# A hybrid decoder step on one core: page and score buffers shared, page numbers read ahead, and a shorter page queue

## The chip, the core and the metric

The kernel runs on one core of a Trainium2 chip. A core has TensorE for matrix products (PE in the profile, PEld where it loads weights), VectorE (DVE), ScalarE (ACT), GpSimd (POOL) and SyncE (SP). SP issues nearly all transfers between HBM and the on-chip SBUF; sixteen DMA engines carry them out. The metric is the time of one execution on the device, in microseconds, as the median of several runs.

## What is computed

One layer of a decoder for a prompt of 256 tokens and, at the same time, 8 requests of 8 new tokens each with 2048 cached positions. One input projection of the 320 rows feeds three branches, and one output projection with a layer norm closes the layer:

```python
aq, ak, av, ag, iq, ik, iw, bq, bf, bi, bg, mq, mg = _in_proj(hs, w_in[l], pos_s)
a_out = _dsa_sample(aq, ak, av, iq, iw, ik, cache_k[l], cache_v[l], cache_idx_k[l], page_table)
b_o, s_s = _hgrn2(bq, bf, bi, lb, state_hgrn[l], t_s)
m_out = _mem_attend(mq, cache_mem_k[l], cache_mem_v[l])
hs_next = _merge(hs, a_out, ag, b_o, bg, m_out, mg, hgrn_norm_g[l], w_out[l], ln_g[l], ln_b[l])
```

The first branch is sparse attention: an indexer scores all cached positions, each query keeps the best 256 and attends over them. Keys, values and indexer keys of the cache lie in pages of 128 positions; `page_table` says which physical page holds which part of a request. The second branch is a gated linear recurrence, the third an attention over 256 memory tokens. The prompt goes through the same steps without a cache.

## The kernel before, in words

**Weights.** The input projection runs as 65 blocks of output columns, each in two halves of 512 KB (`wspec`, loaded by `load_w` into three `wr` buffers). Each half is split into a high and a low part (`prep`), and TensorE makes three products for each piece, xh by high, xl by high, xh by low. Behind the 53rd block lie 16 steps for the prompt's memory keys and values (`in_wm` with `in_memT`), the memory projections of the text below. The output projection, `in_wo`, comes last.

**Pages.** The 8 requests go in 4 pairs. For each pair p there are 8 units of keys (K0 to K3 in `PAGES`), then 8 units of values (V0 to V3); a unit (`unit`) uses two tiles of 1 MB, each with two pages of 512 KB, so 32 pages for a pair's keys and 32 for its values, 256 in all, and 16 more tiles' halves for the cached memory keys and values (XK, XV). A key unit multiplies padded queries with the pages and writes scores to the PSUM bank `kv`; every second unit ScalarE copies them into the score tile S[p]. `soft` turns S[p] into probabilities and frees it; a value unit multiplies these with its pages into the bank `va`. One run of such products, one or two units, between projections is a visit. Page tiles have the tag `pg` with 6 buffers, score tiles the tag `S` with 2. Both tags hold other things at other times: the input and the first weights at the start, the indexer keys (`idx_load`, tiles `ci`) until the indexer is done, the residual and norm tables at the end.

**Page numbers.** `load_pages` asks `page(e)` for a physical number: SP reads it from the table in SBUF into a register (`value_load`, with bounds 0 to 159 that are asserted), works out the address and issues the transfer.

**What sets the order.** The program order of all engines is set when the kernel is built. The class `Plan` keeps, for each engine, the queue of SP and the DMA engines, a time up to which it is planned, and for every tile when it will be written and read. Every instruction goes through `Engine.call`, which issues it and adds its planned cost; a value load costs SP 0.65, transfers run at 380 KB per us (L134). The main loop (L1958 on) lets TensorE always take the next piece that the plan holds for ready: a pair of units whose pages have landed by the plan, or the next quarter of a weight half; one unit alone if the next projection isn't ready or after a time of patience. Background work of the other branches comes in between. `loads` decides what SP issues next: first weights, if a `wr` buffer is free by the plan, then outputs, then pages, if one of 6 buffers is free, the unit is at most 2 ahead of the one that TensorE is at, and less than 8 us of transfers are planned ahead. On the chip each instruction waits for semaphores, so an instruction that the plan put too early makes its engine wait, and SP works strictly in order.

Of the kernel before, what the change touches and what calls it, by code (L numbers as in the profile page):

```python
# [27 lines left out]
PAST = 2048  # L28
# [15 lines left out]
HASTE = 2.0  # L44
CALM = 4.0
IDLE = 3.0
TABLES = {AF.Exp: "exp_ln", AF.Ln: "exp_ln", AF.Silu: "silu", AF.Sqrt: "sqrt"}
EXP_LN = 6
PORT = ("tensor_tensor", "tensor_add", "tensor_sub", "tensor_mul", "scalar_tensor_tensor", "tensor_scalar", "tensor_copy",
# [93 lines left out]
class Engine:  # L143
# [3 lines left out]
    def __getattr__(self, op):  # L147
        f = getattr(self.raw, op)
        plan, eng = self.plan, self.name

        def call(*a, **k):
            if op == "activation":
                self.load_set(TABLES.get(a[2]))
            res = f(*a, **k)  # L154
            aps = [x for x in a if isinstance(x, bass.AP)]
            outs = [v for n, v in k.items() if n in ("out", "accum_out") and isinstance(v, bass.AP)]
            ins = [v for n, v in k.items() if n not in ("out", "accum_out") and isinstance(v, bass.AP)]
            if "out" not in k and aps:
                outs.append(aps.pop(0))
            ins = aps + ins  # L160
            if op == "value_load":
                plan.t[eng] = max(plan.t[eng], plan.now) + 0.65
            elif op == "dma_start":
                plan.dma(eng, outs[0], ins[0])
            elif op == "indirect_dma_start":
                plan.dma(eng, k["out"], k["in_"])
            elif outs:
                n = max(math.prod(x.shape[1:]) for x in outs + ins)
                plan.run(eng, self.cost(op, outs, ins, n), outs, ins,
                         op in PORT and all(x.space != bass.MemoryType.PSUM for x in outs + ins))  # L170
            return res

        return call
# [52 lines left out]
def hymba_step(ctx: ExitStack, tc: tile.TileContext, I, O):  # L226
    nc = tc.nc
    plan = Plan()
# [4 lines left out]
    ctx.enter_context(tc.manual_schedule())  # L233

    uid = [0]
    BUFS = {"t": 17, "s8": 10, "pg": 6, "bp": 2, "wr": 3, "wh": 4, "wl": 4, "S": 2, "row": 4, "mA": 2, "mB": 2, "pj": 2}

    def new(shape, tag, dt=F32, p=None):
        uid[0] += 1
        bufs = BUFS.get(tag, 1)  # L240
        t = (p or pool).tile(shape, dt, name=f"{tag}_{uid[0]}", tag=tag, bufs=bufs)
        plan.slot(tag, bufs, t.tensor.name)
        if tag in ("t", "bp"):
            live[t.tensor.name] = [tag, 1]
        return t
# [18 lines left out]
    def room(k, tag="t", spare=0):  # L264
        while not has_room(k, tag, spare() if callable(spare) else spare):
            yield
# [325 lines left out]
    def prep(i, j):  # L592
# [8 lines left out]
        raw = WR[i][:, w * j:w * j + w]  # L601
        if s.get("res") and kept.index(i) < HOMES:
            if not spare_w:
                for cols, tag in ((2880, "cat0"), (2240, "cat1"), (2320, "PT"), (2048, "pg"), (2048, "pg")):
                    t = new([128, cols], tag, F32R)
                    plan.split.add(t.tensor.name)
                    spare_w.extend(t[:, 512 * k:512 * k + 512] for k in range(4))
            hi, lo = spare_w.pop(0), spare_w.pop(0)
        elif "pair" in s:
            hi, lo = s["pair"]  # L610
        elif s.get("acc") == "rest":
            if j == 0:
                s["bp"] = [new([128, 1024], "bp", F32R) for _ in range(2)]
            hi, lo = (t[:, w * j:w * j + w] for t in s["bp"])
        else:
            hi, lo = new([128, 512], "wh", F32R), new([128, 512], "wl", F32R)
            held["w"] += 1
            s["held"] = True
# [16 lines left out]
    PG = {}  # L635

    def page(e):
        return SP.value_load(ptab[0:1, e:e + 1], min_val=0, max_val=159)

    def load_pages(n, b):  # L640
        kind, p, u = punits[n]
        t = new([128, 2, 1024], "pg")
        PG[n, b] = t
        for j in range(2):
            if kind in ("XK", "XV"):
                SP.dma_start(t[:, j, :], I["c" + kind][4 * p + 2 * b + j])
            else:
                e = (2 * p + b) * 16 + 2 * u + j
                SP.dma_start(t[:, j, :], I["c" + kind.lower()][bass.ds(page(e), 1)].rearrange("o p c -> p (o c)"))

    def pair(x, hp):

# [4 lines left out]
    def unit(n):  # L657
        kind, p, u = punits[n]
        tl = [PG.pop((n, b)) for b in range(2)]
        if kind == "K":  # L660
            if u == 0:
                S[p] = new([128, PAST + NS], "S")
            if u % 2 == 0:
                st["kv"] = PS([128, 512], "kv")
            c = 256 * (u % 2)
# [46 lines left out]
    def unit_ready(n):  # L712
# [2 lines left out]
            return False  # L715
        if kind == "K":
            return u % 2 or ("aq", 7) in done and plan.slot_free("kv", 1) <= plan.now and (
                u or plan.slot_free("S", BUFS["S"]) <= plan.now and len(S) + ci_live(1) < BUFS["S"]
                and (p < BUFS["S"] or ("soft", p - BUFS["S"]) in done))
        if kind == "V":  # L720
            return ("soft", p) in done and plan.avail(PTt[p]) <= plan.now and (u < 7 or "attn" in done) and (
# [46 lines left out]
            yield  # L768

    def ci_live(k):  # L770
        return sum([0, 1, 0, 1][p] == k and ("ci", p) in st for p in range(4))

    def idx_load():

# [1 line left out]
        t = -9.0  # L776
        for sp in range(2):
            for p in (2 * sp, 2 * sp + 1):
                st["ci", p] = x = new([128, PAST], ("pg", "S")[p % 2])
                plan.split.add(x.tensor.name)  # L780
            for c in range(2):
                for f in (1, 0):
# [65 lines left out]
    def idx_sample():  # L848
# [44 lines left out]
        def stack(k):  # L893
# [8 lines left out]
            for j in range(2):  # L902
                own, other = slice(64 * j, 64 * j + 64), slice(64 - 64 * j, 128 - 64 * j)
                ACT.copy(kk[j][own], raw[own])
                DVE.tensor_sub(kk[j][other], raw[own], kk[j][own].bitcast(F32))
            if (c, f) == (1, 0):
                del st["ci", 2 * sp + a]
            return kk

# [200 lines left out]
    def soft(p):  # L1110
# [33 lines left out]
        ps = PS([128, 128])  # L1144
        PE.transpose(ps, Sp[:, PAST - 64:], ident)
        ACT.copy(PTt[p][:, 16, :], ps)
        del S[p]
        done.add(("soft", p))

# [53 lines left out]

    def cross_prompt(h):
        yield from wait("mem", ("mq", h), "attn")
        yield from room(4)
        yield need(MQ[h], st["mkT"][h])
        ps = PS([128, 2, 256])
        for tt in range(2):
# [1 line left out]
        s8 = T8()  # L1211
        DVE.tensor_reduce(s8[:, 0:2], ps, axis=AX.X, op=OP.max)
        DVE.tensor_scalar(s8[:, 2:4], s8[:, 0:2], -QS, None, op0=OP.mult)
        P = [T(256), T(256)]
        pts = [T(256), T(256)]
        free(MQ.pop(h), st["mkT"][h])
        for tt in range(2):
            ACT.activation(P[tt], ps[:, tt, :], AF.Exp, bias=s8[:, 2 + tt:3 + tt], scale=QS,
                           accum_out=s8[:, 4 + tt:5 + tt])
# [6 lines left out]
        for nt in range(2):  # L1226
            for tt in range(2):
                PE.transpose(pt[:, nt, tt, :], P[tt][:, 128 * nt:128 * nt + 128], ident)
        free(*P)
        for nt in range(2):  # L1230
            ACT.copy(pts[nt], pt[:, nt].rearrange("p a b -> p (a b)"))
        yield need(*pts)
# [668 lines left out]
    def loads():  # L1901
        nonlocal nw, npg
        while True:
# [17 lines left out]
                SP.dma_start(dst, src)  # L1921
                continue
            n, b = divmod(npg, 2)
            if (half > 46 and n < len(punits) and len(PG) + ("q" in st) + ("more" in st) + ci_live(0) < BUFS["pg"] and n <= nunit + 2
                    and plan.slot_free("pg", BUFS["pg"]) <= plan.now + 0.2 and plan.t["DMA"] < plan.now + 8):
                load_pages(n, b)
                npg += 1
                continue
# [4 lines left out]
            if n == len(punits) and nunit == n and half > n_in - 6 and ("r", 2) not in st:  # L1933
                ln_load(2)
                continue
            return

    def prep_ready(i, j):
# [175 lines left out]
```

## Time and profile before

| what | value |
|---|---|
| median of 3 runs | 876.76 us (876.49 to 877.36) |
| profiled execution, its own time | 878.17 us |
| profiled execution, span from the first to the last instruction | 876.4 us |
| granted clock of TensorE, mean | 0.998 |
| bytes moved | 266.55 MB, mean 304 GB/s |
| page transfers of keys and of values | 128 and 128, 512 KB each |

The span of one execution in 40 equal slices of 21.9 us: the busy share of each engine in tenths, where 9 is 90% or more, the share of the 16 DMA engines, and what they moved:

```profile
PE   9999999999999999999999999999999999999996
PEld 8999898878988998879888786777888878788885
DVE  6778989748789984645745563585444333943655
ACT  6445666545463444435545364444444433744432
POOL 0543562255644461322433142334222000613424
DMA  8555544899999975999999999999998999876633
GB/s 309 182 165 160 158 144 146 300 342 405 362 410 337 372 260 161 339 411 354 398 367 399 412 377 401 405 347 383 325 408 331 350 384 384 295 269 200 192 101 120
```

TensorE is busy throughout but for the last slice. The DMA engines have three phases: half busy while the indexer runs (to about 150 us), nearly full while pages are read (to about 740 us) with one dip in the sixteenth slice, and falling while the output projection runs. Most groups in this profile carry line 154, since every instruction is issued there; they are told apart by tile names, out<-in.

### The profile page before, as it was taken

To read this page: it belongs to the slowest core of one execution; us is meant where nothing else is said; L and a number is where in the kernel's file an instruction comes from. 1 tells how busy PE (TensorE), PEld (TensorE's weight loads), DVE (VectorE), ACT (ScalarE), POOL (GpSimd) and SP (SyncE) were. 2 spreads that over 40 slices of the span, in tenths; PEclk is the share of its full clock that TensorE was granted. 3 is DMA by queue.
4 is the path that set the end of the run, shared out by engine and by line. 5 is a ranking of instruction groups with operands and counts; after the bars stand their busy time and mean duration, and the time that the engine had idled before them with its cause. 6 is when DMAs were issued, how large, how long until landed. Compare 5 with 4: busy or idle time off the path is not lost.

```text
span 876.4 us, 19974 instructions
## 1 busy us (share of the span) xinstructions
PE 860.5 (98%) x6972; PEld 730.7 (83%) x6974; DVE 558.0 (64%) x1128; ACT 423.0 (48%) x909; POOL 311.7 (36%) x310
## 2 busy tenths in 40 slices
PE   9999999999999999999999999999999999999996
PEld 8999898878988998879888786777888878788885
DVE  6778989748789984645745563585444333943655
ACT  6445666545463444435545364444444433744432
POOL 0543562255644461322433142334222000613424
PEclk9999999999999999999999999999999999999999
DMA  8555544899999975999999999999998999876633
GB/s 309 182 165 160 158 144 146 300 342 405 362 410 337 372 260 161 339 411 354 398 367 399 412 377 401 405 347 383 325 408 331 350 384 384 295 269 200 192 101 120
DMA packets 84375, 266.55 MB, mean 304 GB/s; under 512 B 10609, under 2 KB 21810, under 8 KB 83634
## 3 DMA queue, kind: packets, MB, share of 16 engines
q1 hardware_dynamic: 83250, 263.18, 81.3%
q0 software_dynamic: 1024, 2.10, 0.8%
q8 instruction: 55, 0.90, 0.4%
q14 instruction: 46, 0.38, 0.1%
HBM read 256.50 MB, written 8.73 MB: 303 GB/s over the span
## 4 chain that ended last, share of the span: by engine, by line
PE 91%; DMA 3%; DVE 2%; ACT 1%; SPq 1%; issue 1%; DVEq 0%; ACTq 0%
PE pj L154 53%; PE mB L154 11%; PE va L154 10%; PE mA L154 9%; PE kv L154 7%; DMA pg<-in_ck 2%; SPq L154 1%; ACT wh L154 1%; DVE wl L154 1%; DMA pg<-in_xT 1%; DVE t L154 1%; DMA wr<-in_wt 0%; DVE pg L154 0%; ACT t L154 0%; DVE cat L154 0%
## 5 line engine op out<-in xcount | busy, mean ns | idle before, releaser
L154 PE MATMUL pj<-xh,wh 128*128 128x320 f32 x1008 | 321.9, 319 | 0.0
L154 PE MATMUL pj<-xh,wl 128*128 128x320 f32 x1008 | 311.5, 309 | 0.0
L154 PE MATMUL pj<-xl,wh 128*128 128x320 f32 x1008 | 311.3, 309 | 0.0
L154 ACT CAST wh<-wr 128x512 fp32r<-128x512 f32 x338 | 205.4, 618 | 210.9 <-PE pj L154 155.3
L154 DVE TENSOR_TENSOR wl<-wr,wh 128x512 fp32r<-128x512 f32 x231 | 178.2, 785 | 183.1 <-ACT wh L154 180.2
L154 POOL TENSOR_TENSOR wl<-wr,wh 128x512 fp32r<-128x512 f32 x107 | 145.2, 1362 | 296.8 <-ACT wh L154 272.9
L154 PEld LDWEIGHTS pj<-xh,wh 128*128 128x128 f32 x1008 | 189.4, 188 | 18.4 <-issue 12.7
L154 PEld LDWEIGHTS pj<-xl,wh 128*128 128x128 f32 x1008 | 189.5, 188 | 1.3
L154 PEld LDWEIGHTS pj<-xh,wl 128*128 128x128 f32 x1008 | 189.2, 188 | 0.0
L154 POOL TENSOR_TENSOR t<-t,t 128x320 f32<-128x320 f32 (+3 forms) x44 | 41.1, 935 | 88.5 <-DVE t L154 41.2
L154 PE MATMUL kv<-pg,qpad 128*32 128x256 f32 x1032 | 62.7, 380 | 3.4 <-DMA pg<-in_ck 3.4
L154 PE MATMUL va<-pg,PT 128*32 128x512 f32 x512 | 59.6, 596 | 0.0
L154 PEld LDWEIGHTS kv<-pg,qpad 128*32 128x32 f32 x1032 | 33.4, 110 | 27.2 <-issue 5.7
L154 PEld LDWEIGHTS va<-pg,PT 128*32 128x32 f32 x512 | 15.1, 109 | 30.5 <-issue 29.3
L154 DVE MAX8 PT<-PT 128x8 f32<-128x1032 f32 x32 | 39.5, 1234 | 0.5
L154 DVE MATCH_REPLACE8 PT<-PT 128x1032 f32<-128x1032 f32 x32 | 39.0, 1217 | 0.0
L154 ACT ACTIVATE t<-t 128x320 f32<-128x320 f32 (+1 forms) x44 | 18.5, 455 | 24.7 <-DVE t L154 24.4
L154 POOL TENSOR_TENSOR t<-t,tabm 128x320 f32<-128x320 f32 x16 | 14.0, 878 | 39.1 <-DVE t L154 35.4
L154 POOL DMA_INDIRECT pg<-in_ci,row x16 | 16.6, 1040 | 26.8 <-DVE row L154 19.9
L154 DVE TENSOR_TENSOR t<-t,t 128x320 f32<-128x320 f32 (+4 forms) x28 | 17.6, 629 | 13.4 <-ACT t L154 6.9
L154 ACT ACTIVATE S<-kv 128x512 f32<-128x512 f32 x16 | 9.6, 598 | 32.6 <-PE kv L154 32.6
L154 PE MATMUL mB<-t,wh 128*128 128x256 f32 x128 | 24.0, 286 | 0.0
(360 smaller groups left out, 1314.1 us busy)
## 6 DMA issues: line engine op xcount, KB each, us to landing
pg<-in_ck SPq DMA_DIRECT2D x128, 512.0 KB
pg<-in_cv SPq DMA_DIRECT2D x128, 512.0 KB
wr<-in_wt SPq DMA_DIRECT2D x126, 512.0 KB
wr<-in_wo SPq DMA_DIRECT2D x36, 512.0 KB
wr<-in_wm SPq DMA_DIRECT2D x16, 512.0 KB
pg<-in_cXK SPq DMA_DIRECT2D x8, 512.0 KB
pg<-in_cXV SPq DMA_DIRECT2D x8, 512.0 KB
pg<-in_xT SPq DMA_DIRECT2D x8, 320.0 KB
```

Of the source, the lines that this page charges most:

```text
L154: res = f(*a, **k)
```

## The change

- The tag `pg` has 5 buffers and `S` 3, instead of 6 and 2. A new function, `page_tag`, says whether the next unit's tile can be had and from which tag: `pg` first, else `S`, if a score tile is not held for scores that are live or for those of a pair whose keys are about to begin. Tiles in use are pinned, so that the plan doesn't count them as free.
- The indexer's four key tiles lie once in `pg` and three times in `S`, instead of twice each.
- Units may be loaded 3 ahead (`LOOK`), not 2, and pages are issued only with less than 4 us of transfers planned ahead, not 8.
- Page numbers can be read ahead: `numbers_ahead` reads those of the next two tiles into registers when SP has nothing to do; `load_pages` uses a number that is there. The bounds, and with them the assertion, are gone. The plan counts 0.45 for a value load, not 0.65.
- One tile of the kept output weights lies in `S` and not in `pg`.
- The prompt's memory attention (`cross_prompt`) no longer asks for four free tiles at its start, and takes two of them later.

```diff
+LOOK = 3
-                plan.t[eng] = max(plan.t[eng], plan.now) + 0.65
+                plan.t[eng] = max(plan.t[eng], plan.now) + 0.45
-    BUFS = {"t": 17, "s8": 10, "pg": 6, "bp": 2, "wr": 3, "wh": 4, "wl": 4, "S": 2, "row": 4, "mA": 2, "mB": 2, "pj": 2}
+    BUFS = {"t": 17, "s8": 10, "pg": 5, "bp": 2, "wr": 3, "wh": 4, "wl": 4, "S": 3, "row": 4, "mA": 2, "mB": 2, "pj": 2}
...
-        return SP.value_load(ptab[0:1, e:e + 1], min_val=0, max_val=159)
+        return SP.value_load(ptab[0:1, e:e + 1])
+    def page_tag(n):
+        if n > nunit + LOOK:
+            return None
+        if (len(PG) - len(in_s) + ("q" in st) + ("more" in st) + ci_live(0) < BUFS["pg"]
+                and plan.slot_free("pg", BUFS["pg"]) <= plan.now + 0.2):
+            return "pg"
+        ahead = sum(kind == "K" and u == 0 for kind, _, u in punits[nunit:n + 1])
+        if (len(S) + len(in_s) + ci_live(1) + ahead + sum(("r", m) in st for m in range(2)) < BUFS["S"]
+                and plan.slot_free("S", BUFS["S"]) <= plan.now + 0.2):
+            return "S"
+        return None
+    def numbers_ahead():
+        for m in range(npg, npg + 2):
+            n, b = divmod(m, 2)
+            if n < len(punits) and punits[n][0] in "KV":
+                for j in range(2):
+                    if (n, b, j) not in numbers:
+                        numbers[n, b, j] = number(n, b, j)
+                        return
     def load_pages(n, b):
-        t = new([128, 2, 1024], "pg")
+        tag = page_tag(n)
+        t = new([128, 2, 1024], tag)
...
-                e = (2 * p + b) * 16 + 2 * u + j
-                SP.dma_start(t[:, j, :], I["c" + kind.lower()][bass.ds(page(e), 1)].rearrange("o p c -> p (o c)"))
+                e = numbers.pop((n, b, j)) if (n, b, j) in numbers else number(n, b, j)
+                SP.dma_start(t[:, j, :], I["c" + kind.lower()][bass.ds(e, 1)].rearrange("o p c -> p (o c)"))
...
-                st["ci", p] = x = new([128, PAST], ("pg", "S")[p % 2])
+                st["ci", p] = x = new([128, PAST], "S" if p else "pg")
...
-        yield from room(4)
...
-            if (half > 46 and n < len(punits) and len(PG) + ("q" in st) + ("more" in st) + ci_live(0) < BUFS["pg"] and n <= nunit + 2
-                    and plan.slot_free("pg", BUFS["pg"]) <= plan.now + 0.2 and plan.t["DMA"] < plan.now + 8):
+            if half > 46 and n < len(punits) and page_tag(n) and plan.t["DMA"] < plan.now + 4:
...
+            if half > 40 and plan.t["SP"] <= plan.now:
+                numbers_ahead()
```

How the order changes is shown at three places, from the order in which the built programs hold each engine's instructions. On SP, the first key pages, before (`TENSOR_LOAD ptab` reads a page number, `ISA` rows are register operations, `in_ck` is the cache of keys, `in_wt` the input weights):

```order
L154 DMA wr_2566<-in_wt 128x1024
L154 TENSOR_LOAD ptab
L154 ISA x3
L154 DMA pg_2610<-in_ck 128x1024
L154 TENSOR_LOAD ptab
L154 ISA x3
L154 DMA pg_2610<-in_ck 128x1024
L154 DMA wr_2647<-in_wt 128x1024
```

The same place of the changed kernel:

```order
L155 TENSOR_LOAD ptab x3
L155 DMA wr_1909<-in_wt 128x1024
L155 DMA wr_1973<-in_wt 128x1024
L155 DMA wr_2016<-in_wt 128x1024
L155 DMA wr_2072<-in_wt 128x1024
L155 DMA wr_2126<-in_wt 128x1024
L155 ISA
L155 DMA pg_2170<-in_ck 128x1024
L155 ISA
L155 DMA pg_2170<-in_ck 128x1024
L155 ISA
L155 DMA pg_2173<-in_ck 128x1024
```

The numbers are read among the weights ahead of the pages, each page has one register row and not three, and two tiles are issued before the next weight, not one.

On SP, among the value pages (`in_cv`) of pair 0, where scores of two pairs are live; before:

```order
L154 DMA pg_5111<-in_cv 128x1024
L154 DMA out_vT<-t_5132 128x320
L154 DMA wr_5184<-in_wt 128x1024
L154 DMA wr_5222<-in_wt 128x1024
L154 DMA out_vT<-t_5224 128x320
L154 DMA wr_5273<-in_wt 128x1024
L154 DMA wr_5313<-in_wt 128x1024
L154 DMA out_vT<-t_5315 128x320
L154 DMA wr_5384<-in_wt 128x1024
L154 DMA wr_5435<-in_wt 128x1024
L154 DMA wr_5491<-in_wt 128x1024
L154 DMA wr_5535<-in_wt 128x1024
```

and after:

```order
L155 DMA out_vT<-t_4153 128x320
L155 ISA
L155 DMA S_4184<-in_cv 128x1024
L155 ISA
L155 DMA S_4184<-in_cv 128x1024
L155 TENSOR_LOAD ptab x2
L155 DMA wr_4215<-in_wt 128x1024
L155 DMA wr_4250<-in_wt 128x1024
L155 DMA out_vT<-t_4252 128x320
L155 DMA wr_4302<-in_wt 128x1024
L155 DMA wr_4353<-in_wt 128x1024
L155 DMA wr_4399<-in_wt 128x1024
```

Where weights alone were issued, two pages now go into a score tile; behind these rows a second score tile is filled, and value pages go on two weights later.

On TensorE, the first two units of K3, in the memory projections (`mB` and `pj` are their banks, `qpad` the padded queries); before:

```order
L154 MATMUL mB_8943<-t_9579,wl_9584 128x256
L154 MATMUL kv_9681<-pg_9442,qpad_495 32x256 x2
L154 MATMUL kv_9681<-pg_9501,qpad_495 32x256 x2
...
L154 MATMUL pj_8944<-wh_9602,t_9606 128x512
L154 MATMUL pj_8944<-wh_9602,t_9607 128x512
...
L154 MATMUL kv_9681<-pg_9554,qpad_495 32x256 x2
L154 MATMUL kv_9681<-pg_9652,qpad_495 32x256 x2
```

and after:

```order
L155 MATMUL mB_7299<-t_7721,wl_7749 128x256
L155 MATMUL kv_7845<-pg_7545,qpad_469 32x256 x2
L155 MATMUL kv_7845<-pg_7622,qpad_469 32x256 x2
...
L155 MATMUL kv_7845<-pg_7635,qpad_469 32x256 x2
L155 MATMUL kv_7845<-pg_7691,qpad_469 32x256 x2
...
L155 MATMUL pj_7300<-wh_7762,t_7766 128x512
```

The first unit stands between the same two steps of the memory projections as before; the second unit, which was a visit of its own some steps later, now follows at once.

More of the change, by code (lines that the diff above doesn't have):

```diff
@@ L603, in prep @@
             if not spare_w:
-                for cols, tag in ((2880, "cat0"), (2240, "cat1"), (2320, "PT"), (2048, "pg"), (2048, "pg")):
+                for cols, tag in ((2880, "cat0"), (2240, "cat1"), (2320, "PT"), (2048, "pg"), (2048, "S")):
                     t = new([128, cols], tag, F32R)
@@ L637, in page, with number @@
     def page(e):
-        return SP.value_load(ptab[0:1, e:e + 1], min_val=0, max_val=159)
+        return SP.value_load(ptab[0:1, e:e + 1])
+    in_s = set()
+    def page_tag(n):
[9 more added lines that the diff above has]
+        return None
+    numbers = {}
+    def number(n, b, j):
+        p, u = punits[n][1:]
+        return page((2 * p + b) * 16 + 2 * u + j)
+    def numbers_ahead():
[6 more added lines that the diff above has]
+                        return
     def load_pages(n, b):
         kind, p, u = punits[n]
-        t = new([128, 2, 1024], "pg")
+        tag = page_tag(n)
+        t = new([128, 2, 1024], tag)
         PG[n, b] = t
+        if tag == "S":
+            plan.pinned.add(t.tensor.name)
+            in_s.add((n, b))
         for j in range(2):
@@ L659, in unit @@
         tl = [PG.pop((n, b)) for b in range(2)]
+        plan.pinned.difference_update(t.tensor.name for t in tl)
+        in_s.difference_update([(n, 0), (n, 1)])
         if kind == "K":
@@ L662, in unit @@
                 S[p] = new([128, PAST + NS], "S")
+                plan.pinned.add(S[p].tensor.name)
             if u % 2 == 0:
@@ L717, in unit_ready @@
             return u % 2 or ("aq", 7) in done and plan.slot_free("kv", 1) <= plan.now and (
-                u or plan.slot_free("S", BUFS["S"]) <= plan.now and len(S) + ci_live(1) < BUFS["S"]
+                u or plan.slot_free("S", BUFS["S"]) <= plan.now and len(S) + len(in_s) + ci_live(1) < BUFS["S"]
                 and (p < BUFS["S"] or ("soft", p - BUFS["S"]) in done))
@@ L770, in ci_live @@
     def ci_live(k):
-        return sum([0, 1, 0, 1][p] == k and ("ci", p) in st for p in range(4))
+        return sum([0, 1, 1, 1][p] == k and ("ci", p) in st for p in range(4))
     def idx_load():
@@ L778, in idx_load @@
             for p in (2 * sp, 2 * sp + 1):
-                st["ci", p] = x = new([128, PAST], ("pg", "S")[p % 2])
+                st["ci", p] = x = new([128, PAST], "S" if p else "pg")
+                plan.pinned.add(x.tensor.name)
                 plan.split.add(x.tensor.name)
@@ L906, in stack @@
             if (c, f) == (1, 0):
+                plan.pinned.discard(st["ci", 2 * sp + a].tensor.name)
                 del st["ci", 2 * sp + a]
@@ L1146, in soft @@
         ACT.copy(PTt[p][:, 16, :], ps)
+        plan.pinned.discard(S[p].tensor.name)
         del S[p]
@@ L1213, in cross_prompt @@
         DVE.tensor_scalar(s8[:, 2:4], s8[:, 0:2], -QS, None, op0=OP.mult)
+        free(MQ.pop(h), st["mkT"][h])
         P = [T(256), T(256)]
-        pts = [T(256), T(256)]
-        free(MQ.pop(h), st["mkT"][h])
         for tt in range(2):
@@ L1229, in cross_prompt @@
         free(*P)
+        pts = [T(256), T(256)]
         for nt in range(2):
```

## The prediction

> **What bounds the kernel now.** I read the page's header and its chain first, then what TensorE waits for, then those waits in the order of time, then the DMA share by stage, and last the SP queue ahead of the longest of those waits.
>
> ```profile
> span 876.4 us, 19974 instructions
> PE 860.5 (98%) x6972; PEld 730.7 (83%) x6974; DVE 558.0 (64%) x1128; ACT 423.0 (48%) x909; POOL 311.7 (36%) x310
> PE 91%; DMA 3%; DVE 2%; ACT 1%; SPq 1%; issue 1%; DVEq 0%; ACTq 0%
> ```
>
> TensorE is busy for 860.5 of 876.4 us and has 91% of the chain that ended last. The change does not alter one matrix product: the program order of both kernels holds the same number of matmuls, with the same shapes. So the end can only move by what TensorE loses between them: 876.4 - 860.5 = 15.9 us of idle time, and the small gaps that come with a change of work. A view of TensorE's waits names the larger pieces:
>
> ```profile
> PE kv L154 <- DMA pg<-in_ck: 3.4, 4, 1.6
> PE pj L154 <- issue: 1.4, 1, 1.4
> ```
>
> Columns: time lost in all, how often, the longest. Key pages that had not landed cost 3.4 us in four waits; one wait of 1.4 us has no releaser that the profile shows. Nearly all the rest of the 15.9 us lies before the first projection and behind the last output product; neither is touched. TensorE's timeline shows where the four waits are:
>
> ```profile
> 596.78 1.92 PE L154 MATMUL kv<-pg,qpad 128*32 128x256 f32 x28 [0.58 <-DMA pg<-in_ck]
> 604.19 1.71 PE L154 MATMUL kv<-pg,qpad 128*32 128x256 f32 x26 [0.53 <-DMA pg<-in_ck]
> 613.67 1.92 PE L154 MATMUL kv<-pg,qpad 128*32 128x256 f32 x28 [0.72 <-DMA pg<-in_ck]
> 637.05 1.92 PE L154 MATMUL kv<-pg,qpad 128*32 128x256 f32 x28 [1.57 <-DMA pg<-in_ck]
> ```
>
> All four lie between 596 and 637 us, at the keys of the last request pair (K3), during and just behind the memory projections. In each case the first four products of a unit ran and the other 28 stood: the planner had started a unit whose second tile it held for landed. The transfers by stage (start:end, TensorE busy, its clock, DMA share, GB/s):
>
> ```profile
> 330.00:350.00 20.00, 20.00 (x149) 1.00 0.56 168
> 350.00:525.00 175.00, 174.84 (x1688) 1.00 0.98 382
> 525.00:555.00 30.00, 28.59 (x320) 1.00 1.02 402
> 595.00:640.00 45.00, 41.28 (x517) 1.00 0.97 364
> ```
>
> From 350 us on the DMA engines are full, and only the last stretch pays for it. Just before, there is a hole: 20 us at a share of 0.56. SP's timeline shows why, and what one page costs that queue:
>
> ```profile
> 329.62 15.06 SPq L154 DMA_DIRECT2D wr<-in_wt  x5
> 345.45 6.34 SPq L154 DMA_DIRECT2D pg<-in_cv  x6
> 601.80 3.70 SPq L154 DMA_DIRECT2D pg<-in_ck  x4
> ```
>
> From 329.62 for 15.06 us it issues weights alone: every page buffer is full. At 601.80 four pages take 3.70 us from the first issue to the end of the fourth.
>
> **The change part by part.**
>
> *Page numbers.* The chain of waits shows one page on SP between two issues, in pieces (0.04 to 0.06 us between them left out), and what follows the last issue:
>
> ```profile
> 601.80 0.33 SPq L154
> ...
> 602.17 0.28 SPq L154
> ...
> 602.50 0.15 SPq L154
> ...
> 602.70 0.02 SPq L154
> ...
> 602.76 0.04 SPq L154
> ...
> 602.90 10.63 DMA pg<-in_ck
> ```
>
> Issue, load of the page number, a register operation, an assertion, the address; from 601.80 to the next issue at 602.90 is 1.10 us. Two of the three register rows go (the bounds of the value load): I take the 0.15, the 0.02 and their two gaps, near 0.27 us a page. In the changed order 160 of the 256 numbered pages have no load directly ahead of them, so these cost SP a further 0.28 + 0.05 = 0.33 us less at that moment. None of this is on TensorE. SP is at the head of the chain only here, and behind its last issue stand 10.63 us of landing, about eight pages of queue at 3.70 / 4 = 0.9 us an issue or, by bytes, 512 KB / 402 GB/s = 1.30 us each. An earlier issue into a full queue lands no earlier. Worth by itself: between 0 and the idle share of that stretch, 3% of 45 us = 1.4 us; I take 0, as it can only show in the page waits, which are counted next.
>
> *Buffers.* Two score tiles still hold S[0] and S[1] in the hole, so the third, and a freed one, take pages there. Counted in SP's order up to the first load of the memory weights, 178 pages have been issued where 168 were; up to the sixteenth, 202 in both. So between these two loads 24 pages are issued and not 34: 10 x 512 KB = 5.2 MB, 13 us of transfers at 402 GB/s, leave the full stretch and go into the hole, which has 0.44 x 20 = 8.8 us of room, and the weights-only issue ahead of it. 13 us is far more than the 3.4 us that the waits cost. But the planner starts a unit as soon as it takes its pages for landed, and K3's units stand at nearly the same place between the projections as before, so the head start is used up by then; what is left is a queue that is shorter when K3's pages enter it. The gain lies between 0 and 3.4 us. I take two of the four waits' smaller size as staying, 0.53 x 2 = 1.1 us, and so a gain of **2.3 us**: nearer to the upper end, since the bytes removed are several times the lateness.
>
> *Visits.* TensorE leaves the projections for a visit to the pages, and pays for it:
>
> ```profile
> 336.87 6.16 PE pj L154 x42
> 343.04 3.57 PE va L154 x32
> 346.61 6.36 PE pj L154 x42
> ```
>
> 42 projection matmuls take 6.16 us undisturbed and 6.36 behind a visit: 0.20 us each time. In TensorE's order the page visits fall from 43 to 41, since more units find their partner loaded: 0.4 us. Other interruptions stay within one of their old number.
>
> *Shorter page queue* (4 us of planned transfers ahead, not 8). The same bytes move; pages wait in HBM and not in the queue, and weights find a shorter one. The longest wait of a projection for its weights, in the view of TensorE's waits, is this:
>
> ```profile
> PE pj L154 <- DVE pg L154: 0.2, 1, 0.2
> ```
>
> 0.2 us, once, so there is nothing to gain there. What it can lose is the first rival below; in the sum it is 0.
>
> *The 1.4 us without a releaser* stands in the chain right behind a burst of tiny products of the recurrence:
>
> ```profile
> 538.50 1.42 PE mA L154 x108
> 539.91 1.35 PE pj L154 x5
> 541.26 1.41 issue
> ```
>
> There is one burst a head, four in both kernels, in other surroundings now; the wait may go, stay or come twice: -1.4 to +1.4 us, taken as 0.
>
> *Index keys and memory attention.* Three of the four index tiles now lie in score buffers; their transfers are of the same size, and TensorE never waited for them. The probabilities' transposes of the memory attention take their two tiles later and need no four free tiles at the start; the work is the same and lies under projections. Both at 0.
>
> Sum: 2.3 + 0.4 = 2.7 us. The profiled execution took 878.17 us, 1.8 outside its span; it would take 875.5. It lay 1.4 us above the median of the three runs, 876.76, and none of the terms depends on that difference, so the median goes to **874.0 us**.
>
> **The rivals.**
>
> *The lateness only moves (no change).* What makes a page late is not the bytes but the planner's rate against the real one: it counts 380 GB/s (L134), and the stretch with the waits moved 364. The missing 4% of 45 us is 1.9 us of lateness, whatever came before, and K3's units are still started the moment they are taken for landed. Then waits of 3.4 - 0.5 us remain, and the time is 876.76 - 0.9 = about 875.9. For it: the units stand at nearly the same places. Against: 350 to 525 ran at 382 and 525 to 555 at 402, faster than planned, so the lateness arises in the last stretch alone, the one from which the pages go. [...]
>
> *A queue that runs short (slower).* A page let in only when 4 us are planned ahead has less cover for its landing. The chain shows what a 512 KB load takes where the engines are about half idle:
>
> ```profile
> 77.90 4.10 DMA wr<-in_wt
> ```
>
> 4.10 us, as much as the whole new limit. If the planner's queue is empty earlier than the real landing, each visit from the memory projections to the end of K3 waits, seven in the changed order (two of V2, five of K3). At the mean of the four old waits, 0.85 us, that is 6.0 us in place of 3.4: 2.6 slower, less 0.4 for the visits, 876.76 + 2.2 = 879.0. It decides once the page waits exceed 3.4 + 0.4 + 1.8 = 5.6 us. Against it: a page's transfer is 1.30 us, so 4 us are three pages, and the real queue was longer than planned.
>
> *The change doesn't do what it says.* 96 pages still load their number directly ahead, 14 of the 34 numbered pages around the memory projections among them. Since SP's share was taken as 0, this changes no term.
>
> **How the numbers follow.** A measurement of this kernel can tell about 0.2% (1.75 us) from no change, so faster means below 875.0. The forecast and its neighbours below that have 0.52; the middle case, waits that stay or a gain that another small wait eats, 0.29; the slower case 0.19. Lower end: all page waits (3.4), the visits (0.4) and the unexplained wait (1.4) gone, 871.5, and a little for waits too small to be listed: 871.2. Upper end: the slower rival's 879.0, which leaves half of it out.
>
> **What would show it.** In TensorE's waits the row of kv for pages falls to about 1 us, or rises past 5.6 if the queue runs short. The hole near 330 us closes (share above 0.8), with value pages read from score tiles. SP shows under 0.9 us between pages of one run. The count of TensorE instructions stays at 6972 within missing records. The prediction is wrong if waits appear at the values (va) or at weights where there were none, or if the recurrence's bursts stall more than once.

## The result and the profile after

The changed kernel takes **884.6 us** (median of six runs, 881.78 to 887.54) beside 877.03 for the kernel before (876.49 to 878.01) in the same series: a ratio of 1.0082 with an interval of [1.0059, 1.0105]. It is slower by 0.8%; 874.0 was forecast, and the time lies above the range. The profile below is of the shortest of the six executions (881.78 us): its span is 3.5 us longer than that of the profile before, where the medians differ by 7.6, so its rows show a part of the loss only.

The header of the changed kernel's page and its chain, in the order in which those of before were shown:

```profile
span 879.9 us, 19334 instructions
PE 861.0 (98%) x6974; PEld 730.0 (83%) x6974; DVE 559.4 (64%) x1125; ACT 422.3 (48%) x909; POOL 318.6 (36%) x313
PE 81%; DVE 8%; DMA 3%; issue 2%; ACT 1%; SPq 1%; POOL 0%; DVEq 0%; ACTq 0%; POOLq 0%
```

TensorE's work is the same (861.0 us, 6974 instructions), but its share of the chain falls from 91% to 81%, and VectorE's rises from 2% to 8%: the end is now set in part by engines that TensorE waits for. (A share of the chain is not time lost: TensorE is busy for 98% of the span in both.) What it waits for (time in all, how often, the longest):

```profile
PE mB L155 <- DVE s L155: 1.5, 2, 1.2
PE mA L155 <- DVE cat L155: 1.5, 2, 1.2
PE mA L155 <- ACT t L155: 1.2, 1, 1.2
...
PE kv L155 <- DMA pg<-in_ck: 0.9, 2, 0.8
PE mA L155 <- ACT xh L155: 0.9, 1, 0.9
...
PE pj L155 <- issue: 0.5, 1, 0.5
```

In this execution the forecast's own row did what it should: pages cost 0.9 us where they cost 3.4, and the wait without a releaser 0.5 where it was 1.4. The hole is partly closed too, though not to the share above 0.8 that was to show it (stage, TensorE busy, clock, DMA share and GB/s among the columns):

```profile
330.00:350.00 20.00, 20.00 (x152) 16.32 (x154) 7.52 (x22) 9.63 (x18) 5.08 (x4) 1.00 0.71 250
```

0.71 and 250 GB/s stand where there were 0.56 and 168. The loss is in rows that the kernel before does not have. TensorE's timeline of the changed kernel gives their places:

```profile
41.71 0.93 PE L155 MATMUL mA<-t,t 64*128 64x128 f32 x8 [1.21 <-DVE cat L155]
...
655.12 0.38 PE L155 MATMUL mB<-maskb,emat 128*128 128x512 bf16 x1 [1.18 <-DVE s L155]
...
657.57 0.66 PE L155 MATMUL mA<-csm,t 128*128 128x64 f32 x4 [1.24 <-ACT t L155]
...
753.02 0.49 PE L155 MATMUL mA<-wh,xh 128*128 128x512 f32 x1 [0.87 <-ACT xh L155]
754.03 0.50 PE L155 MATMUL mA<-wh,xl 128*128 128x512 f32 x1 [0.51 <-POOL xl L155]
...
769.59 0.50 PE L155 MATMUL mA<-wl,xh 128*128 128x512 f32 x1 [0.48 <-DVE wl L155]
```

At the place of the first row, the kernel before has this:

```profile
40.55 0.93 PE L154 MATMUL mA<-t,t 64*128 64x128 f32 x8 [0.17 <-DVE cat L154]
```

There are three places: the start of the index scores (1.2 us near 42 us, where the kernel before waited 0.17), the softmax of a request pair beside the cross-attention and the recurrence (1.18 + 1.24 = 2.4 us near 655), and the start of the output projection (0.87 + 0.51 + 0.48 = 1.9 us). Two more show in other runs: the mask near 321 us (0.3 here, 1.3 elsewhere) and a varying page wait.

Each place suggests a cause. *Output projection:* in the kernel before, the last values stood directly ahead of the first output product:

```profile
739.91 6.45 PE pj L154 x44
746.36 4.43 PE va L154 x40
750.79 0.89 PE mA L154 x3
```

For 4.43 us TensorE did products of values while ScalarE, VectorE and GpSimd split the heads' outputs into xh and xl. In the changed kernel that visit comes 24 products earlier (it starts at 743.52, and avS is the last value tile of it), projections follow it, and nothing covers the split:

```profile
746.98 1.04 PE L155 MATMUL va<-avS,PT 128*32 128x512 f32 x8
```

*Softmax:* ScalarE's timeline, the two exponentials of cross_prompt, first before, then after:

```profile
653.04 0.47 ACT L154 ACTIVATE t<-mB,s 128x256 f32<-128x256 f32 x1 [1.87 <-DVE s L154]
...
653.50 0.47 ACT L154 ACTIVATE t<-mB,s 128x256 f32<-128x256 f32 x1
```

```profile
651.73 0.47 ACT L155 ACTIVATE t<-mB,s 128x256 f32<-128x256 f32 x1 [2.66 <-DVE s L155]
...
656.20 0.47 ACT L155 ACTIVATE t<-mB,s 128x256 f32<-128x256 f32 x1 [3.90 <-PE mA L155]
```

They stood back to back; now the second waits 3.90 us for a product of TensorE, which itself stands behind the mask product that waits at 655.12. Each end of this knot holds the other. cross_prompt is the function in which the change dropped the request for four free tiles and moved the allocation.

### The profile page after: what moved, and what is told of

Read it like the earlier page. It is cut to its first block, busy times and chain, and to the rows that moved or that the text cites. A ratio compares the mean times of both kernels' runs of the same rounds, so it can differ in the third digit from the quotient of the medians.

```text
span 879.9 us, 19334 instructions
## 1 busy us (share of the span) xinstructions
PE 861.0 (98%) x6974; PEld 730.0 (83%) x6974; DVE 559.4 (64%) x1125; ACT 422.3 (48%) x909; POOL 318.6 (36%) x313
## 4 chain that ended last, share of the span: by engine, by line
PE 81%; DVE 8%; DMA 3%; issue 2%; ACT 1%; SPq 1%; POOL 0%; DVEq 0%; ACTq 0%; POOLq 0%
PE pj L155 46%; PE mB L155 11%; PE va L155 9%; PE mA L155 9%; PE kv L155 7%; DVE PT L155 4%; DMA pg<-in_ck 2%; DMA wr<-in_wt 1%; DVE t L155 1%; DVE wl L155 1%; SPq L155 1%; ACT wh L155 0%; DVE pg L155 0%; DVE cat L155 0%; DVE bp L155 0%
## 5 line engine op out<-in xcount | busy, mean ns | idle before, releaser
L155 DVE TENSOR_TENSOR wl<-wr,wh 128x512 fp32r<-128x512 f32 x225 | 174.6, 786 | 204.2 <-ACT wh L155 190.5
L155 POOL TENSOR_TENSOR wl<-wr,wh 128x512 fp32r<-128x512 f32 x113 | 154.3, 1371 | 270.1 <-ACT wh L155 240.6
L155 POOL TENSOR_TENSOR t<-t,t 128x320 f32<-128x320 f32 (+3 forms) x41 | 38.1, 930 | 104.2 <-ACT t L155 47.4
L155 PE MATMUL kv<-pg,qpad 128*32 128x256 f32 x900 | 60.0, 380 | 0.9 <-DMA pg<-in_ck 0.9
L155 PEld LDWEIGHTS kv<-pg,qpad 128*32 128x32 f32 x900 | 31.5, 110 | 23.9 <-issue 2.5
L155 POOL DMA_INDIRECT S<-in_ci,row x24 | 24.9, 1036 | 30.1 <-DVE row L155 22.6
L155 DVE TENSOR_TENSOR t<-t,t 128x320 f32<-128x320 f32 (+4 forms) x31 | 20.2, 650 | 7.3 <-POOL t L155 6.2
```

## The experiments

Theory in all of them: the time is lost at these separate places, by the moved order and by what the change took out, and not in the transfers. Rivals: the loss is scatter of a job; the shorter queue starves; the repairs share one slack.

| kernel | median us (lowest to highest, runs) | ratio to before, interval |
|---|---|---|
| changed kernel, again | 885.11 (882.34 to 886.41, 6) | 1.0086 [1.0071, 1.0100] |
| + values held back | 882.04 (879.84 to 885.67, 6) | 1.0065 [1.0048, 1.0082] |
| + cross-attention as before | 881.49 (879.35 to 882.85, 6) | 1.0048 [1.0034, 1.0062] |
| + both repairs | 877.08 (876.29 to 879.75, 12) | 1.0007 [0.9997, 1.0017] |
| + index tiles exchanged, alone | 882.21 (881.57 to 883.52, 5) | 1.0066 [1.0053, 1.0079] |
| + all three | 877.26 (876.12 to 881.31, 11) | 1.0009 [0.9998, 1.0020] |
| changed, queue 8 us | 882.96 (881.42 to 883.28, 5) | 1.0069 [1.0056, 1.0082] |
| both repairs, bounds back | 882.46 (881.27 to 885.66, 6) | 1.0072 [1.0057, 1.0087] |
| both repairs, old buffers | 882.50 (881.53 to 882.89, 5) | 1.0063 [1.0050, 1.0076] |
| three repairs, queue 8 us | 887.95 (887.56 to 888.29, 4) | 1.0128 [1.0113, 1.0143] |
| three repairs, queue 6 us | 877.93 (876.62 to 879.72, 11) | 1.0011 [1.0002, 1.0020] |
| **kernel before, no bounds** | 876.29 (875.37 to 877.79, 12) | 0.9991 [0.9982, 0.9999] |

The rows come from three jobs (1 to 3 and 12; 4 to 7; 8 to 11), in which the kernel before had medians of 877.19, 876.94 and 876.89. The changed kernel itself ran in the first of them only, so a difference to it from another job is rough, and the ratios are the safer measure.

### Again, unchanged

> The changed kernel once more, to see whether its scatter (881.8 to 887.5 us in six runs, where the kernel before lies within 1.5 us) belongs to it. Theory A (fixed stalls: the new order loses the same 3 to 4 us in every run, and the runs above that met a disturbed chip): five runs within 1.5 us of each other, 880 to 883. Theory B (the new order stands on waits that a little lateness makes longer, so the time depends on how the transfers fall): again a spread of over 3 us, mean near 884.5, with a lower granted clock in the longer runs.

885.11: the loss and its width (4 to 6 us where the kernel before has 1.5 to 3.3) belong to the kernel, as theory B said. The profile of this second series (span 884.7 us, TensorE busy 863.0) is 4.8 us longer than the first: page waits of 3.2 us in place of 0.9, 1.3 at the mask in place of 0.3, and 1.7 us lost to a lowered clock (last section) make 5.0, and some small waits are shorter.

### The last values held back

```diff
-            return ("soft", p) in done and plan.avail(PTt[p]) <= plan.now and ...
+            return (n < len(punits) - 2 or half >= n_in) and ("soft", p) in done and plan.avail(PTt[p]) <= plan.now and ...
```

> The changed kernel with one visit moved: the last two value units wait for the last projection, so that they stand between the projections and the output projection as in the kernel before; nothing ahead of that place is moved. Theory A1 (the last visit was the cover for splitting the branch outputs into high and low parts): TensorE's waits for ACT xh, POOL xl and DVE wl around 752 to 769 us go, and 2.0 to 2.4 us with them against the changed kernel. Rival (the stall only moves to the first weights of the output projection or comes from their late transfer): less than 0.5 us is won.

882.04, 3.1 us less than the changed kernel in the same job; between the means it is 2.6, and the ranges overlap, so the size is rough. The chain there reads as before again, the values directly ahead of the first output product and no wait for xh, xl or wl behind them:

```profile
747.83 4.43 PE va L155 x40
752.26 0.89 PE mA L155 x3
```

### Cross-attention as before

```diff
         yield from wait("mem", ("mq", h), "attn")
+        yield from room(4)
         yield need(MQ[h], st["mkT"][h])
...
+        P = [T(256), T(256)]
+        pts = [T(256), T(256)]
         free(MQ.pop(h), st["mkT"][h])
-        P = [T(256), T(256)]
...
-        pts = [T(256), T(256)]
```

> The changed kernel with the prompt's memory attention as before (four free tiles asked for at its start, two of them not taken late). The order is the same up to that attention. Theory A2 (without that request its exponentials are issued into tiles that are still being read, ScalarE stands for 3.9 us at about 656 us and TensorE behind it): the two waits of 1.2 us at 653 to 658 us go, 2 to 2.5 us. Rival (those waits come from the masks of the last key pair falling together with the recurrence, and not from the tiles): they stay, and the time is within 0.7 us of the changed kernel.

881.49, 3.6 us less, between the means too. The mask products and the prefix product run through:

```profile
652.19 0.38 PE L155 MATMUL mA<-maskb,emat 128*128 128x512 bf16 x1 [0.16 <-PE mA L155]
652.41 0.38 PE L155 MATMUL mB<-maskb,emat 128*128 128x512 bf16 x1
653.55 0.61 PE L155 MATMUL mA<-csm,t 128*128 128x64 f32 x4
```

The request for room and the place of the allocation were undone together, and either moves the order of the products by itself; which of the two does it is open.

### Both repairs

> The changed kernel with both repairs tried apart: the last two visits of values are held back until the last projection, and the cross-attention of the prompt asks for room and takes its tiles in the order of before. Theory A, the two losses are separate waits at separate places (2.4 us of pitch at 752 to 769 us, 2.4 us at 653 to 658 us, and the half clock that sometimes follows the latter): the gains add, 885.1 less 3.1 less 3.6 gives 878.4 us (877.4 to 879.6), and both groups of waits are gone from the profile. Theory B, both repairs work by giving back the same slack, to the page transfers or to the clock: the gains do not add, and the time stays at 881 to 882 us.

877.08, 8.0 us less than the changed kernel of the first job: the gains add (3.1 + 3.6 = 6.7, and somewhat more). The theory of one shared slack falls. The kernel is now level with the one before.

### The index tiles exchanged

```diff
-                st["ci", p] = x = new([128, PAST], "S" if p else "pg")
+                st["ci", p] = x = new([128, PAST], "pg" if p == 1 else "S")
```

(and ci_live counts accordingly). The matmuls stand in the same order. Of the changed kernel, GpSimd's and VectorE's timelines near the wait at 42 us:

```profile
30.98 1.29 POOL L155 DMA_INDIRECT pg<-in_ci,row  x1 [6.81 <-ACT wh L155]
...
36.45 0.96 POOL L155 MEMSET avS<- 64x1024 f32 x1
37.35 0.58 POOL L155 MEMSET t<- 128x256 f32 x2
```

```profile
36.37 2.00 DVE L155 STREAM_SHUFFLE t<-pj 128x320 f32<-128x320 f32 x1
```

With one page buffer fewer, the first index tile takes a slot that ScalarE's split of weights had used, and the first load waits for ScalarE and not for its row numbers alone. GpSimd's memsets end at 37.93 (before: 36.76), and the shuffle beside them takes 2.00 us (before: 0.97), ending 0.4 us behind them in both kernels.

> The changed kernel with the index tiles of the first two page halves exchanged between the two pools (the first in a score buffer, the second in a page buffer); the order of the matmuls is the same to the row. In the changed kernel GpSimd's first index load waits for a page slot that ScalarE had in use, its memsets end 1.2 us later, the shuffle on VectorE beside them takes 2.00 us in place of 0.97, and TensorE waits 1.2 us for it near 42 us. Theory A: that 1.2 us wait goes and, nothing behind it being short, stays gone: 883.9 us beside 885.1 of the changed kernel. Theory B: the wait goes, but the lead is lost where page transfers are short (587 to 640 us), so no gain: 885.1 us. If the wait near 42 us stays, its cause is another.

> All three repairs in one: values held back, cross-attention with room, index tiles exchanged. Theory A (separate losses that add): 877.2 us, 1.2 below the kernel with two repairs and level with the kernel before (877.0 to 877.2); what is left against the forecast of 874.0 is then in waits that the kernel before did not have (mask at 321 us, 1.3) and in the page waits that remain. Theory B (one shared slack): 881 to 882 us.

In the run with the exchange alone the tile's wait went, and the first load starts at 30.57, but GpSimd's next sum took 1.28 us (0.75 in the changed kernel), the memsets end at 37.64, and the shuffle still takes 1.50. TensorE waits 0.70 us there, and as long in the run with all three:

```profile
41.46 0.93 PE L155 MATMUL mA<-t,t 64*128 64x128 f32 x8 [0.70 <-DVE cat L155]
```

0.5 us of the 1.2 came back at the place. (In the profile with all three and a queue of 8 us, whose order up to there is the same, the wait is 0.17 as in the kernel before.) In the time it can't be told: 882.21 alone is under both theories, but the changed kernel did not run in that job, and its own shortest runs took 881.78 and 882.34; and 877.26 was had with all three where it was 877.08 with two. So the slot is part of the cause there, and the gain too small to show.

### Page numbers: the bounds taken from the kernel before, and put back into the repaired one

```diff
-        return SP.value_load(ptab[0:1, e:e + 1], min_val=0, max_val=159)
+        return SP.value_load(ptab[0:1, e:e + 1])
```

> The kernel before with the bounds of the value load taken away and nothing else; all engines keep their order, SP alone has two register rows less for each number. By the prediction SP is not on TensorE's path but for the page waits at 596 to 637 us: 0 to 1.4 us faster. If SP's slowness is what makes these pages late: 1.5 to 3.4 us faster, with the page waits gone. Slower by over 0.5 us is expected by none.

> The kernel with two repairs (values held back, cross-attention with room), with one part of the change undone: the page numbers are loaded with their bounds again, as before, so that each of SP's loads takes two register rows more (about 0.27 us). The order is the same on every engine. Theory A, the saved register rows are what lets the pages come earlier (they alone took the waits of the kernel before from 3.4 to 1.2 us): page waits of 3.4 us or more at 587 to 640 us, and 878.0 to 880.0 us beside 877.1 with the repairs alone. Theory B, numbers loaded ahead and more places for pages suffice: page waits of 2 to 2.5 us and 876.6 to 877.6 us.

Neither run moves an instruction on any engine, but for SP's own two register rows a page. In the kernel before, the page waits fall to one, and its stage moves 390 GB/s in place of 364:

```profile
598.16 1.92 PE L154 MATMUL kv<-pg,qpad 128*32 128x256 f32 x28 [1.25 <-DMA pg<-in_ck]
```

876.29 us, and the only kernel here whose interval lies below 1, by a hair. In the repaired kernel the bounds cost 5.4 us (5.7 by the ratios, since the two runs are of different jobs), more than either theory said. SP's timeline shows how, first without, then with bounds:

```profile
620.13 2.37 SPq L155 DMA_DIRECT2D out_mkT<-t  x3
...
625.53 1.07 SPq L155 DMA_DIRECT2D pg<-in_ck  x2
```

```profile
621.32 2.88 SPq L155 DMA_DIRECT2D out_mkT<-t  x3
...
628.84 0.90 SPq L155 DMA_DIRECT2D pg<-in_ck  x2
```

The same pages are issued 3.3 us later. The first 1.6 us had gathered by the last result ahead of them (624.72 for 623.08) and are not taken apart here. The other 1.7 come where SP reads three page numbers ahead, in front of a weight and the pages: that takes 1.3 us without the bounds and 3.0 with them, of which the bounds' own rows are 1.1 and slower loads 0.6 (the first took 1.17 us, not 0.34). So numbers read ahead can delay the pages when SP is already late. The stage table (without, then with bounds) shows that the transfers then run short:

```profile
625.00:632.00 7.00, 7.00 (x217) 6.76 (x217) 1.99 (x3) 1.82 (x4) 0.00 (x0) 1.00 1.04 404
```

```profile
625.00:632.00 7.00, 7.00 (x199) 6.81 (x201) 2.23 (x4) 2.08 (x4) 0.00 (x0) 1.00 0.86 276
...
636.00:640.00 4.00, 3.37 (x28) 1.58 (x28) 0.00 (x0) 0.00 (x0) 0.00 (x0) 0.58 1.02 418
```

and TensorE stands for it:

```profile
PE kv L155 <- DMA pg<-in_ck: 5.5, 3, 3.8
```

5.5 us where the repaired kernel had 2.5: 3.0 us. The other part is in the clock of the last row above: taken for 1.00 or 0.50 (0.50 is a whole row of the run with the 6.5 us wait below), 0.58 over 4 us is an estimate of (1 - 0.58) x 4 / 0.5 = 3.4 us at half speed, right behind the wait of 3.8 us, and half of it, 1.7 us, is lost. 3.0 + 1.7 = 4.7 us, the difference of the spans (880.3 - 875.6).

### The queue of pages

```diff
-            if half > 46 and n < len(punits) and page_tag(n) and plan.t["DMA"] < plan.now + 4:
+            if half > 46 and n < len(punits) and page_tag(n) and plan.t["DMA"] < plan.now + 8:
```

> The changed kernel with the queue of pages as long as before (a page is asked for while under 8 us of transfers are queued, not 4). The order of visits moves with it. Theory A, the losses come from the order of the work and not from the queue: 883 to 887 us, with page waits as in the changed kernel (0.9 to 3.2 us). Theory B, the short queue lets the transfers run dry and costs the changed kernel its time: 877 to 880 us, with the page waits at 587 to 640 us gone.

> The kernel with three repairs and the queue of pages of before (8 us, not 4). Theory A, a longer queue takes the page waits that are left (2.0 us) and the repairs keep the rest: 875.0 to 875.6 us, 0.2% under the kernel before. Theory B, as with the longer queue alone, the moved order puts new waits at projections near 540 to 580 us (about 3 us) in place of the page waits: 877 to 879 us.

> As the run with the queue of 8 us, at 6 us. If the length of the queue itself mattered, the time would lie between those at 4 and at 8 us; if the order that comes out of it matters, it can lie outside: 875 to 880 us.

With 8 or 6 us no wait for key pages is listed any more, as theory B of the first run said. Yet the changed kernel stays at 882.96, at the edge of what its theory A said, for the order moves with the limit, and new waits of projections come in (1.0 for GpSimd, 0.9 for VectorE, 0.8 for ScalarE), beside those at the output projection. So the short queue does leave pages late, by 1 to 3 us, and curing it in this way gains nothing that these runs can tell. On top of the three repairs 6 us gives 877.93, and 8 us gives 887.95, far outside what was expected: one wait of 6.5 us for xh at the start of the output projection. The stage table of that run:

```profile
750.00:757.00 7.00, 0.50 (x5) 0.11 (x1) 2.23 (x4) 2.74 (x6) 0.09 (x1) 0.71 0.84 344
757.00:762.00 5.00, 4.71 (x11) 3.33 (x12) 4.85 (x9) 5.00 (x16) 4.47 (x6) 0.50 0.86 220
762.00:770.00 8.00, 8.00 (x36) 6.58 (x35) 8.00 (x15) 6.71 (x24) 7.19 (x9) 0.92 0.85 309
```

TensorE stands for most of 7 us and then works at half clock (0.50 from 757 to 762 us). ScalarE's timeline shows why xh is so late:

```profile
754.12 2.41 ACT L155 CAST wh<-wr 128x512 fp32r<-128x512 f32 x4 [14.36 <-DMA wr<-in_wo]
```

The split of xh, at 756.44, stands behind these four splits of output weights, which had not landed. SP issued the weights from 748.30 only. It had stood for 17.8 us, to 747.88, for value products that read a score buffer, because it was to load the residual there and the weights come behind in its order. With all three repairs and 4 us the same load goes out at 736.08. Values held back, value pages in score buffers and this order together make the wait.

### The buffers as before

```diff
-    BUFS = {"t": 17, "s8": 10, "pg": 5, ..., "S": 3, ...}
+    BUFS = {"t": 17, "s8": 10, "pg": 6, ..., "S": 2, ...}
```

(The kept output weights and the index tiles lie in the buffers of before, no pages in score buffers; both repairs are kept.)

> The kernel with two repairs, with another part of the change undone: six page and two score buffers as before, pages in page buffers only, index tiles in the pools of before; numbers ahead, no bounds, short queue stay. Visits stand nearly as in the kernel before (43 of them, the hole at 330 to 350 us open). Theory A, the new buffers brought the waits at 42 us (1.0) and at the mask near 321 us (0.7) and saved 2 visits (0.4) and some page waits: without them 876 to 876.8 us and those two waits are gone. Theory B, the buffers carry the gain in page waits: those return to 3.4 us or more, and the time is 878 to 879 us.

882.50, which neither theory gives. The wait at 42 us is gone (0.17), as the first said, so it does come with the buffers and the index tiles in them; the wait for the mask stays (1.0 us), so that one comes with the order. Page waits are 2.3 us at the keys, 0.7 at the values, and a new wait of 1.8 us stands before the memory's products near 546 us. From about 205 us on at the latest the order differs from every other kernel's, so the 5.4 us against the repaired kernel can't be put down to the buffers themselves. One thing can be read from it: the hole is open again (share 0.48 from 330 to 350 us, 0.71 in the repaired kernel), and yet the keys wait no longer than the 2.5 us of the repaired kernel (one profile of each).

## Why the prediction was wrong

**The page waits, 2.3 us.** The size looks right in the first profile, 3.4 to 0.9 us with 1.1 forecast to stay, but that is in part luck: the row varies (0.9 and 3.2 us in two profiles of the changed kernel, 2.5 and 2.0 with two and three repairs). It is not a number of the kernel but of an execution. The mechanism, fewer late pages because the hole takes some of them, is not shown: the hole did fill in part, but with the hole open and the buffers of before the keys wait 2.3 us, not more than with both repairs.

**Page numbers, taken as 0 within 0 and 1.4 us.** Mis-sized, and for a wrong reason. "An earlier issue into a full queue lands no earlier" read an average share of 0.97 as a queue full at every moment. SP itself is late around 590 to 640 us, where it issues weights, memory inputs, results and pages; without the two register rows alone, and with nothing moved, the waits fell by 2.2 us and the time by 0.9 (877.19 to 876.29, interval of the ratio just below 1). Put back, the bounds cost 3.0 us of waits and 5.4 us in all. So the row of waits fell by nearly as much, with the register rows alone, as was credited to the buffers. The 2.2 us are of two single executions, a long one before (878.17 us) and a short one without bounds (875.44); of the time, 0.9 us is what is shown.

**The step that failed** is the one that set everything else to nothing: that nearly all the rest of the idle time "lies before the first projection and behind the last output product; neither is touched", and that for index tiles and memory attention "the work is the same and lies under projections. Both at 0". The sum took the waits of before and asked which would go. It never asked which new ones the new order would make. TensorE's idle time, 15.9 us before, was 18.9 us in the first profile after and 21.7 in the second:

- the last value visit, 4.43 us of cover for the split ahead of the output projection, was moved 24 products up, and 1.9 us of waits appeared (3.1 us of time by the run that holds it back);
- cross_prompt without its room made a knot of two waits, 2.4 us (3.6 us by the run that restores it);
- the first index tile took a used slot, 1.0 us more at 42 us, of which the exchange brought half back in most profiles; 0.3 to 1.3 us at the mask near 321 us.

The first two could have been read before: the chain of before shows the 4.43 us of values directly ahead of the output products, and the changed order shows projections there instead; and a dropped wait for room means that a tile can lie where another is still read. That it is the tile, and not the order alone, which makes the knot is argued and not shown, since both were undone together.

**Visits, 0.4 us.** Too small beside the rest to be told apart. **The wait without a releaser**: 0.5 to 0.6 us where 1.4 stood, inside its bounds.

**The rivals.** The slower case was put on the short queue; that was the wrong mechanism. Its signature, page waits past 5.6 us, did not come, and the longer queue left the changed kernel at 882.96. The forecast's own signs, a wait "at the values or at weights where there were none", caught only the smallest of them, the 0.5 us for wl: the others are for index scores, the mask, the recurrence and the heads' outputs.

**What is left after both repairs.** The repaired kernel stands at +0.1 us against the kernel before, in the same job, where -2.7 was forecast: 2.8 us to explain. Its profile has 1.0 us more at 42 us (1.2 for 0.17), 1.3 at the mask, and page waits of 2.5 where 1.1 was taken, less 0.8 at the wait without a releaser: 1.0 + 1.3 + 1.4 - 0.8 = 2.9 us. That this fits is in part chance: each row is of one execution, that of the kernel before was over its median, and the spans of the two profiles differ by -0.8 us (875.6 and 876.4), not by +0.1. For the changed kernel itself the rows account for the 2.4 and 1.9 us; the repairs brought 8.0 in the medians and 5.5 to 6.0 in the lowest runs. Part of what is beyond the rows is the half clock of the last section and page waits that vary, and the rest is not assigned.

## What to carry to other kernels

Where a change moves the order, don't stop at which waits of before will go: for each place where a long job of one engine covers a hand-over of the others (here 4.43 us of values ahead of the output projection), look whether it still stands there, and for each dropped wait for room, whose slot the tile will get. An average DMA share near 1 over tens of us did not say here that the queue was full at every moment (0.97 from 595 to 640 us before, with two slices of 1.2 us near 624 at about 0.4); look at when the issuing engine comes to each transfer, and count its register instructions. The edit that needed no new order, two register rows less a page, was the one that paid, and by little: 876.29 us, 0.9991 of before [0.9982, 0.9999].

## What was not expected of the hardware

In three of these profiles TensorE's granted clock fell to about half for some us behind a wait or two. Behind the 3.8 us page wait above it was 3.4 us at half speed; the 28 products there took 3.58 us, where the kernel before took 1.92 for the same 28 (at 637.05). In the run with the 6.5 us wait it was (0.29 x 7 + 0.50 x 5 + 0.08 x 8) / 0.5 = 10.3 us, three times as long. In the second series the profiled run of the changed kernel shows it behind the knot, which there lies at 657 to 661 us:

```profile
655.00:660.00 5.00, 3.29 (x50) 2.12 (x39) 2.00 (x6) 1.11 (x5) 0.00 (x0) 1.00 1.03 405
660.00:665.00 5.00, 4.30 (x17) 3.71 (x18) 1.86 (x9) 2.96 (x5) 0.00 (x0) 0.66 1.03 417
```

That is (1 - 0.66) x 5 / 0.5 = 3.4 us at half speed, and 1.7 us lost. The mask product at 661.20 took 0.61 us, where that of the first profile took 0.38 (at 658.06). TensorE had not stood for several us at a stretch there: its two waits were 1.18 and 1.24 us, with products between them. In the first profile the same two waits are 1.18 and 1.24 us as well, and the clock stays at 1.00 (stage, TensorE busy, clock, DMA share, GB/s):

```profile
650.00:675.00 25.00, 22.59 (x204) 1.00 0.91 337
```

What decides between the two is not shown. Only some executions have a lowered mean clock: 0.996 or less (the profiled run above has 0.995, that of the first series 0.997) was granted in 3 of 6 and 2 of 6 runs of the changed kernel in its two series, in all 6 of the kernel whose profile has the 3.8 us page wait and all 4 of the one with the 6.5 us wait, in none of the 6 with the cross-attention as before and in 1 of 12 with both repairs, but in 4 of 6 where the values alone were held back. So two waits of 1.2 us, whose ends lie 2.45 us apart in both, came with a loss of 1.7 us beyond them in one profile, and with none in the other.
